# Gated channel tiles in pairs, five buffers for them, and a first block product fed in halves

## The chip, the cores and the metric

The kernel runs on one core of a Trainium2 chip. The metric is the device time of one execution in microseconds (us). The engines are TensorE (PE, matrix multiply), VectorE (DVE), ScalarE (ACT), GpSimd (POOL) and SyncE (SP, which only issues transfers); ACT, POOL and SP each have a queue that issues DMA transfers in program order, and each engine runs its instructions in order.

## What is computed

One layer of a hybrid token mixer over 2048 tokens of 1024 channels. Cut to what matters here:

```python
h = rms_norm(x, norm_g) * (1 + scale) + shift
va, za, bb, bc, bv, zb, ca, cg, zc, dv, zd = split(h @ w_in, 11)      # 512 channels each
ya = rglru(va)                                  # A: two scans with gates
yb = bb * conv3(bc * bv)                        # B
u  = layer_norm(conv31(ca * sigmoid(cg)))       # C
yc = silu(u) @ c_pw + c_pw_b
yd = (pool_grid(dv) @ d_w + d_b) * d_scale      # D
cat = concat([ya * silu(za), yb * silu(zb), yc * silu(zc), yd * silu(zd)])
x = x + gate * (cat @ w_out)
return rms_norm(x, final_g)
```

## The kernel before

Tokens are cut into four blocks of 512 (block b), channels into tiles of 128. Every fp32 matmul operand is split into a high and a low part (`split`, L105 to L108: the high part on ACT, the low part on DVE), and three matmuls of 128x128 by 128x512 make one product of parts. An input projection of one channel tile over one block is thus 24 matmuls into one of four PSUM accumulators (pool `pm`). `load_w` brings a tile's weights through the pool `wst` (two slots) and splits them into `wh` and `wl` (pool `wp`, three slots each).

The order of groups is written out in `JOBS`: A to D are the mixers' branches, a lower-case letter is a gated ("z") tile of that branch, F is `finish_c(b)` for one block, G and X, Y are other parts. Behind the list the last two z tiles run together with `project_two`. A scheduler with a simulated clock and priorities (`tc.high_priority(offset=URGENT)`) sets from it the order on each engine and the slot of each tile.

A z tile (`gated`, L461) takes silu of the accumulator on ACT into `sz` (L467), loads the branch's output `yt` on SP's queue (L472), multiplies on DVE (L473) and stores the product to DRAM on POOL's queue (`to_cat`, L455), even tiles into `first`, odd ones into `second`. The output projection is done as seven block products (a Strassen form), which need sums of even and odd tiles' halves. So an odd tile loads its even partner back (`yp`, L477), makes four sums (L479 to L482) in place, and stores them with two transfers (`to_sums`, L459). `sz`, `yt` and `yp` come from the pool `z2` with three slots, 512 floats wide.

`finish_c` (L765) does the layer norm of branch C for one block: it loads `uc`, gets the column mean by a matmul with a constant (`column_mean`: mups L790, and varps for the variance), takes the square root on ACT and the reciprocal on DVE, silu for four pieces, and then 48 matmuls with c_pw (pwps, L814). The first call loads c_pw (`pws`) on ACT's queue through `wst` into four `l4` tiles. The split mean operand `hl` stands in the pool `acc`.

Each of the seven products (L964 on: order 1, 2, 6, 7, 4, 5, 3) runs eight tiles of 24 matmuls (`q`, L995). The right operand `wo` is made of eight pieces (`wos`, `right`), each loaded through `wst`; those of product 1 are requested on ACT's queue (L909), the others on SP's. The left operand of a tile is one load of 512 KB into an `l4` tile (`load_left`, L930), three tiles ahead, and a split into `ahl`. `TILES` orders the eight tiles; tile p belongs to block p // 2. The last steps of the kernel add the residual and normalise.

Of the kernel before, what the change touches and what calls it, by code (L numbers as in the profile page):

```python
# [8 lines left out]
F32 = mybir.dt.float32  # L9
F32R = mybir.dt.float32r  # L10
# [34 lines left out]
def flow_backbone_kernel(  # L45
# [265 lines left out]
    def load_w(slot, q, spare=False, sub=None):  # L311

        col = slot * W + q * P
        res = []
        with tc.high_priority(offset=URGENT):
            for hf in range(2):
                ws = wst_p.tile([P, 4, P], F32, tag="wst", name="ws")
                r = hf * 512
                nc.sync.dma_start(ws, w_in[0, r : r + 512, col : col + P].rearrange("(k p) e -> p k e", p=P))
                if spare and hf == 1:  # L320
                    both = acc_p.tile([P, 2, 4, P], F32R, tag="acc", name="whl")
                    wh, wl = both[:, 0], both[:, 1]
                else:
                    wh = wp.tile([P, 4, P], F32R, tag="wh", name="wh")
                    wl = wp.tile([P, 4, P], F32R, tag="wl", name="wl")
# [24 lines left out]
    def project_two(jobs, before=lambda b: None):  # L350

        ws = [load_w(slot, q, j == 1, nc.gpsimd if len(hb) == 1 else None) for j, (slot, q, _) in enumerate(jobs)]
        for b in range(NB):
# [107 lines left out]
    def gated(g, q):  # L461

        ch = 4 * "abcd".index(g) + q

        def one(b, ps):
            sz = z2("sz")
            nc.scalar.activation(sz, ps, AF.Silu)  # L467
            if g == "c":
                nc.gpsimd.dma_start(y_d[g, q][b // 2][:, 512 * (b % 2) : 512 * (b % 2 + 1)], sz)
                return  # L470
            yt = z2("yt")
            nc.sync.dma_start(yt, y_d[g, q][b // 2][:, 512 * (b % 2) : 512 * (b % 2 + 1)])  # L472
            nc.vector.tensor_tensor(sz, sz, yt, op=MUL)  # L473
            to_cat(b, ch, sz)
            if ch % 2:
                yp = z2("yp")
                nc.sync.dma_start(tokens(yp), first_d[b][:, :, ch // 2, :])  # L477
                x1, y1, x2, y2 = yp[:, :256], yp[:, 256:], sz[:, :256], sz[:, 256:]
                nc.vector.tensor_tensor(yt[:, :256], x1, y1, op=ADD)  # L479
                nc.vector.tensor_tensor(y1, y1, y2, op=ADD)  # L480
                nc.vector.tensor_tensor(x1, x1, y1, op=ADD)
                nc.vector.tensor_tensor(yt[:, 256:], x1, x2, op=ADD)  # L482
                to_sums(b, ch // 2, yp, yt)

        return one

# [278 lines left out]
    def finish_c(b):  # L765
        if not pw:
            for i in range(NQ):
                ws = wst_p.tile([P, W], F32, tag="wst", name="pws")
                load = nc.scalar.dma_start(ws, c_pw[0, i * P : (i + 1) * P, :])
                follow(load, last_act[0], "the tiles of the recurrence are free after its last block")  # L770
                t = l4("pw", F32R, (P, 2, W))
                nc.scalar.activation(t[:, 0, :], ws, AF.Copy)
                nc.vector.tensor_tensor(t[:, 1, :], ws, t[:, 0, :].bitcast(F32), op=SUB)
                pw.append(t)
        if True:
# [6 lines left out]
            def column_mean(name, src, t):  # L782
# [47 lines left out]
            for dst, p0, p1 in ((s3, x1, y1), (s1, y1, y2), (s2, s1, x1), (s4, s2, x2)):  # L830
                nc.vector.tensor_tensor(dst, p0, p1, op=ADD)
# [11 lines left out]
    def z(g, q):  # L843
        project(Z[g], q, gated(g, q))
# [25 lines left out]
    project_two([(ZD, 3, gated("d", 3)), (ZA, 3, gated("a", 3))])  # L870
# [31 lines left out]
    def right(i):  # L902
# [4 lines left out]
        def one(k):  # L907
            ws = wst_p.tile([P, 512], F32, tag="wst", name="wos")
# [58 lines left out]
    TILES = (4, 5, 0, 1, 6, 7, 2, 3)  # L967
    todo = [(i, p) for i in ORDER for p in TILES]
    ats = [load_left(LEFT[i], p) for i, p in todo[:AHEAD]]
    for n, i in enumerate(ORDER):  # L970
# [4 lines left out]
        for m, p in enumerate(TILES):  # L975
            at = ats.pop(0)
            if 8 * n + m + AHEAD < len(todo):
# [75 lines left out]
```

## Time and profile before

| what | us |
|---|---|
| median of three runs | 1530.59 |
| lowest and highest run | 1526.68, 1532.86 |
| the profiled execution | 1526.85 |
| its span in the trace | 1524.9 |
| PE busy, DVE busy, ACT busy, POOL busy | 1453.0, 1116.2, 662.1, 166.7 |
| stretch of z tiles and finish_c, from the first pwps to the first product | 960.0 to 1201.3 |
| the seven products | 1201.3 to 1516.0 |

A time in the trace counts from the start of the span; the profiled execution's own time is 1.95 us longer than its span. "Busy" is the share in which an engine has an instruction under way; a pipelined matmul that follows another adds less than its own duration. A wait is put down to the instruction or transfer that ended it. The stretch of the table was found by the lines: L814 is pwps and L995 the products.

### The profile page before, as it was taken

How to read it: one execution, taken by the hardware profiler on the slowest of the kernel's cores; microseconds unless marked ns; L12 is line 12 of the kernel's file. 1: busy time of each engine (PE TensorE's matmuls, PEld its weight loads, DVE VectorE, ACT ScalarE, POOL GpSimd, SP SyncE). 2: the span in 40 equal slices, each digit the busy share in tenths (PEclk: the TensorE clock that was granted, in tenths of full speed). 3: DMA queues.
4: the chain of work that ended last, by engine and by line, in shares of the span. 5: the costliest groups of instructions: out<-in, count | busy, mean ns of one | idle time of the engine just before them, and what ended most of it. 6: DMA issues, size and time to landing. Idle time of an engine off the chain costs nothing.

```text
span 1524.9 us, 17881 instructions
## 1 busy us (share of the span) xinstructions
PE 1453.0 (95%) x6457; PEld 1184.8 (78%) x6457; DVE 1116.2 (73%) x1573; ACT 662.1 (43%) x949; POOL 166.7 (11%) x290
## 2 busy tenths in 40 slices
PE   5999999999999999999999999979999699999997
PEld 3778888888888888888878887857877587788886
DVE  6889984869966999988844976464547446766897
ACT  7773475543144541343635345332424233333432
POOL 0200000000100000111111001323222210000000
PEclk9999999999999999999999999989999899999999
DMA  9312121322311223223243126646566968775674
GB/s 370 122 52 81 49 87 58 104 89 71 112 38 48 84 69 111 96 102 124 90 159 111 62 97 207 205 147 234 172 215 225 331 200 272 255 233 175 212 251 152
DMA packets 157308, 223.88 MB, mean 147 GB/s; under 512 B 16283, under 2 KB 98211, under 8 KB 157220
## 3 DMA queue, kind: packets, MB, share of 16 engines
q1 hardware_dynamic: 135836, 154.29, 31.9%
q0 software_dynamic: 19648, 65.31, 11.1%
q10 hardware_dynamic: 1736, 3.15, 0.7%
q8 instruction: 50, 0.82, 0.2%
q14 instruction: 38, 0.31, 0.1%
HBM read 149.29 MB, written 73.40 MB: 146 GB/s over the span
## 4 chain that ended last, share of the span: by engine, by line
PE 63%; issue 17%; DMA 11%; POOL 3%; DVE 3%; SPq 1%; ACT 1%; POOLq 0%; DVEq 0%; ACTq 0%
PE ps L342 44%; PE q L995 12%; PE gps L411 3%; PE ps L359 2%; DMA yp<-first 2%; DMA sums<-yp 2%; DMA yt<-yb 2%; SPq L132 1%; POOL sums L459 1%; DMA wos<-in_w_out_dram 1%; DMA sums<-yt 1%; DMA ws<-in_w_in_dram 1%; PE dps L758 1%; PE psc L636 1%; DMA yt<-ya 1%
## 5 line engine op out<-in xcount | busy, mean ns | idle before, releaser
L342 PE MATMUL ps<-hb,wh 128*128 128x512 f32 x2560 | 717.7, 395 | 11.5 <-ACT sz L467 10.8
L342 PEld LDWEIGHTS ps<-hb,wh 128*128 128x128 f32 x2560 | 483.2, 189 | 119.5 <-ACT sz L467 13.0
L342 PE MATMUL ps<-hb,wl 128*128 128x512 f32 x1280 | 411.7, 393 | 0.0
L995 PE MATMUL q<-wo,ahl 128*128 128x512 f32 x1344 | 308.8, 391 | 15.8 <-ACT sz L467 10.0
L995 PEld LDWEIGHTS q<-wo,ahl 128*128 128x128 f32 x1344 | 252.6, 189 | 72.0 <-ACT sz L467 10.4
L342 PEld LDWEIGHTS ps<-hb,wl 128*128 128x128 f32 x1280 | 242.0, 189 | 52.2 <-issue 1.7
L107 ACT ACTIVATE wh<-ws 128x512 fp32r<-128x512 f32 x94 | 58.6, 626 | 159.7 <-PE ps L342 141.6
L473 DVE TENSOR_TENSOR sz<-sz,yt 128x512 f32<-128x512 f32 x48 | 33.0, 687 | 92.3 <-DMA yt<-yd 30.7
L108 DVE TENSOR_TENSOR wl<-ws,wh 128x512 fp32r<-128x512 f32 x91 | 62.1, 684 | 30.2 <-ACT wh L107 30.0
L467 ACT ACTIVATE sz<-ps 128x512 f32<-128x512 f32 x64 | 36.9, 595 | 106.2 <-DVE yt L482 35.2
L539 DVE SCALAR_TENSOR_TENSOR cacc<-vc,csum,cacc 128x1024 f32<-128x1024 f32 x60 | 76.6, 1276 | 0.3
L525 DVE SCALAR_TENSOR_TENSOR cacc<-vc,pt,cacc 128x1024 f32<-128x1024 f32 x60 | 76.7, 1278 | 0.0
L417 ACT ACTIVATE gate<-gps,pt 128x512 f32<-128x512 f32 x64 | 40.9, 687 | 78.2 <-PE gps L411 78.1
L519 DVE SCALAR_TENSOR_TENSOR cb<-vc,pt,cb 128x1024 f32<-128x1024 f32 x56 | 71.8, 1282 | 0.0
L359 PE MATMUL ps<-hb,wh 128*128 128x512 f32 x192 | 64.0, 405 | 4.9 <-ACT sz L467 4.0
L107 ACT ACTIVATE wo<-wos 128x512 fp32r<-128x512 f32 x56 | 34.5, 628 | 69.5 <-DVE wos L913 40.6
L397 DVE SCALAR_TENSOR_TENSOR xc<-va,pt,xc 128x1024 f32<-128x1024 f32 x48 | 61.3, 1277 | 0.2
L913 DVE TENSOR_TENSOR wos<-wos,wot 128x512 f32<-128x512 f32 x40 | 26.8, 690 | 33.2 <-DMA wos<-in_w_out_dram 19.2
L108 DVE TENSOR_TENSOR wo<-wos,wo 128x512 fp32r<-128x512 f32 x56 | 37.3, 687 | 16.5 <-ACT wo L107 15.8
L107 ACT ACTIVATE ahl<-s 128x1024 fp32r<-128x1024 f32 x32 | 33.5, 1054 | 36.3 <-PE q L995 31.3
L426 DVE SCALAR_TENSOR_TENSOR xc<-xc,gate 128x1024 f32<-128x1024 f32 x16 | 19.6, 1224 | 40.6 <-ACT xc L425 40.5
L359 PEld LDWEIGHTS ps<-hb,wh 128*128 128x128 f32 x192 | 36.4, 193 | 13.6 <-ACT sz L467 4.8
(255 smaller groups left out, 1874.1 us busy)
## 6 DMA issues: line engine op xcount, KB each, us to landing
ws<-in_w_in_dram SPq DMA_DIRECT2D x96, 256.0 KB
s<-sums SPq DMA_DIRECT2D x32, 512.0 KB
wos<-in_w_out_dram SPq DMA_DIRECT2D x40, 256.0 KB
wot<-in_w_out_dram SPq DMA_DIRECT2D x40, 256.0 KB
modw<-in_mod_w_dram SPq DMA_DIRECT2D x8, 1024.0 KB
a<-second SPq DMA_DIRECT2D x16, 512.0 KB
xo<-in_x_dram SPq DMA_DIRECT2D x32, 256.0 KB
out_dram<-ys SPq DMA_DIRECT2D x32, 256.0 KB
```

The lines of the kernel that those rows point to most:

```text
L107: nc.scalar.activation(hi, src, AF.Copy)
L108: (sub or nc.vector).tensor_tensor(lo, src, hi.bitcast(F32), op=SUB)
L342: nc.tensor.matmul(ps[u], lhsT=wk, rhs=hb[2 * pr + u][:, k, part, :], start=(k == 0 and n == 0), stop=(k == NK - 1 and n == 2),)
L359: nc.tensor.matmul(ps, lhsT=wk, rhs=hb[b][:, k, part, :], start=(k == 0 and n == 0), stop=(k == NK - 1 and n == 2),)
L397: nc.vector.scalar_tensor_tensor(xc, v[:, o + k : o + k + n], par(w0 + k, q), xc, op0=MUL, op1=ADD)
L411: nc.tensor.matmul(ps, lhsT=w[:, 2 * d + g, :], rhs=xx[:, u : u + m], start=(i == 0), stop=(i == len(terms) - 1))
L417: nc.scalar.activation(dst[:, u : u + m], ps, AF.Sigmoid, bias=par(bias, q))
L467: nc.scalar.activation(sz, ps, AF.Silu)
L519: nc.vector.scalar_tensor_tensor(bb, x1[:, 1 + j : 1 + j + n], odd(j), bb, op0=MUL, op1=ADD)
L525: nc.vector.scalar_tensor_tensor(acc, x0[:, j : j + n], even(j), acc, op0=MUL, op1=ADD)
L539: nc.vector.scalar_tensor_tensor(acc, x1[:, 1 + j : 1 + j + n], csum[:, q, j : j + 1], acc, op0=MUL, op1=ADD)
L995: nc.tensor.matmul(ps, lhsT=hl[:, a, k, :], rhs=wo[:, k, w, :], start=(k == 0 and e == 0), stop=(k == NK - 1 and e == 2))
```

## The change

A z tile of the branches A, B and D no longer stands alone: `z` projects two channel tiles (even and odd) with `project_two`, block after block. The even tile's `sz` and `yt` stay in SBUF until the odd tile of the same block has its product; `pair_sums` then writes the four sums into the two `yt` tiles and reads the two `sz`. No `yp` is loaded. `z2` has five slots. The `wh` and `wl` tiles have four slots, and the spare weight tile in `acc` is gone. `JOBS` is reordered: the pair b0 stands where a single tile of it stood later, the tiles of C move, finish_c runs in the block order F0, a0, F1, F2, F3, and the last pair is a2 with a3. The column mean's two split halves and the four `pws` loads share tiles `gwh` and `gwl` of the pool `gp`, and `pws` is requested on SP's queue. The pieces of product 1's right operand go through `z2` instead of `wst`. Product 1's left operands are loaded as two halves of 256 KB through `wst` and split into `wh` and `wl`; the other products load as before. `TILES` is 0 to 7.

```diff
 JOBS = (
-    "X0 Y0 c0 G6 B0 G1 G5 A0 D1 b0 G3 G0 C1 B1 A1 G7 G2 C2 c1 c2 G4 A2 C3 b1 B2 D0 D2 c3 A3 d0 D3 B3 a0 "
-    "F2 d1 F0 a1 b2 F3 F1 a2 b3 d2"
+    "X0 Y0 c0 G6 B0 G1 G5 A0 D1 c1 G3 G0 C1 B1 A1 G7 G2 C2 b0 G4 A2 C3 c2 B2 D0 D2 c3 A3 d0 D3 "
+    "B3 F0 a0 F1 F2 F3 b2 d2"
 )
+LAST = ("a", 2)
+BLOCKS = (0, 1, 2, 3)
...
-    wp = ctx.enter_context(tc.tile_pool(name="wp", bufs=3))
+    wp = ctx.enter_context(tc.tile_pool(name="wp", bufs=4))
...
-    zp = ctx.enter_context(tc.tile_pool(name="zp", bufs=3))
+    zp = ctx.enter_context(tc.tile_pool(name="zp", bufs=5))
...
+        def chunk(b, ps, e):
+            yt, sz = z2("yt"), z2("sz")
+            nc.sync.dma_start(yt, y_d[g, q + e][b // 2][:, 512 * (b % 2) : 512 * (b % 2 + 1)])
+            nc.scalar.activation(sz, ps, AF.Silu)
             nc.vector.tensor_tensor(sz, sz, yt, op=MUL)
-            to_cat(b, ch, sz)
-            if ch % 2:
-                yp = z2("yp")
-                nc.sync.dma_start(tokens(yp), first_d[b][:, :, ch // 2, :])
...
-                to_sums(b, ch // 2, yp, yt)
+            to_cat(b, ch + e, sz)
+            return yt, sz
+        def first(b, ps):
+            even[b] = chunk(b, ps, 0)
+        def second(b, ps):
+            (s21, s0), (s34, s1) = even.pop(b), chunk(b, ps, 1)
+            pair_sums(s21[:, 256:], s21[:, :256], s34[:, :256], s34[:, 256:], s0[:, :256], s0[:, 256:], s1[:, :256], s1[:, 256:])
+            to_sums(b, ch // 2, s21, s34)
...
+    def pair_sums(s1, s2, s3, s4, x1, y1, x2, y2):
+        for dst, p0, p1 in ((s1, y1, y2), (s2, s1, x1), (s3, x1, y1), (s4, s2, x2)):
+            nc.vector.tensor_tensor(dst, p0, p1, op=ADD)
...
-                ws = wst_p.tile([P, W], F32, tag="wst", name="pws")
-                load = nc.scalar.dma_start(ws, c_pw[0, i * P : (i + 1) * P, :])
+                ws = gp.tile([P, W], F32, tag=f"gw{'hl'[i % 2]}", name="pws")
+                nc.sync.dma_start(ws, c_pw[0, i * P : (i + 1) * P, :])
...
-                hl = acc_p.tile([P, 2, 512], F32R, tag="acc", name="hl")
+                hl = [gp.tile([P, 512], F32R, tag=f"gw{h}", name=f"h{h}") for h in "hl"]
...
-        project(Z[g], q, gated(g, q))
+            first, second = gated(g, q)
+            project_two([(Z[g], q, first), (Z[g], q + 1, second)], blocks=BLOCKS)
...
-    project_two([(ZD, 3, gated("d", 3)), (ZA, 3, gated("a", 3))])
+    z(*LAST)
...
-            ws = wst_p.tile([P, 512], F32, tag="wst", name="wos")
+            ws = z2("wos") if i == 1 else wst_p.tile([P, 512], F32, tag="wst", name="wos")
...
-    TILES = (4, 5, 0, 1, 6, 7, 2, 3)
+    TILES = [2 * b + t for b in BLOCKS for t in range(2)]
...
+    def left_parts(name, p):
+        res = []
+        for hf in range(2):
+            at = wst_p.tile([P, 4, P], F32, tag="wst", name="ah")
+            nc.sync.dma_start(at, left(name, p)[:, 4 * hf : 4 * hf + 4, :])
+            ah = wp.tile([P, 4, P], F32R, tag="wh", name="ahh")
+            al = wp.tile([P, 4, P], F32R, tag="wl", name="ahl")
+            split(ah, al, at)
+            res.append((ah, al))
+        return res
...
-    nc = _bacc.Bacc("TRN2", target_bir_lowering=False, num_devices=1)
+    nc = _bacc.Bacc("TRN2", target_bir_lowering=False, num_devices=1, dynamic_dma_scratch_size=8192)
```

What this does to the order on three engines at the end of the z tiles is shown in pieces of the instruction order. On PE, before, the last z tile (ps1_3_3: branch A's gate, tile 3, block 3) stands directly ahead of product 1, whose tiles q1_4, q1_5 and so on each run as 24 matmuls in one piece:

```order
L359 MATMUL ps1_3_3_8805<-hb3_917,wh_8523 128x512 x2
L359 MATMUL ps1_3_3_8805<-hb3_917,wl_8524 128x512
L359 MATMUL ps1_3_3_8805<-hb3_917,wh_8523 128x512 x2
L359 MATMUL ps1_3_3_8805<-hb3_917,wl_8524 128x512
L359 MATMUL ps1_3_3_8805<-hb3_917,whl_8529 128x512 x12
L995 MATMUL q1_4_8900<-wo1_8847,ahl_8897 128x512 x24
L995 MATMUL q1_5_8935<-wo1_8847,ahl_8932 128x512 x24
L995 MATMUL q1_0_8970<-wo1_8847,ahl_8967 128x512 x24
```

After, the variance matmuls of the last finish_c stand between, and q1_0 and q1_1 alternate by pieces of wo1:

```order
L358 MATMUL ps1_3_3_8769<-hb3_918,wh_8530 128x512 x2
L358 MATMUL ps1_3_3_8769<-hb3_918,wl_8531 128x512
L801 MATMUL varps_7806<-hh_7802,onesm_101 128x512
L801 MATMUL varps_7806<-hl_7803,onesm_101 128x512
L1031 MATMUL q1_0_8875<-wo1_8809,ahh_8846 128x512
L1031 MATMUL q1_1_8917<-wo1_8809,ahh_8865 128x512
L1031 MATMUL q1_0_8875<-wo1_8809,ahh_8846 128x512
L1031 MATMUL q1_0_8875<-wo1_8809,ahl_8847 128x512
L1031 MATMUL q1_1_8917<-wo1_8809,ahh_8865 128x512
L1031 MATMUL q1_1_8917<-wo1_8809,ahl_8866 128x512
L1031 MATMUL q1_0_8875<-wo1_8809,ahh_8846 128x512
```

So product 1 begins with two tiles side by side, and the 48 pwps matmuls of the last finish_c stand further down, between the tiles of product 1.

On ACT, before, wo1's pieces are requested (L909) and split (L107) four z tiles ahead of the last one, sz_8596 being an earlier tile's silu:

```order
L467 ACTIVATE sz_8596<-ps1_3_0_8571 128x512
L909 DMA wos_8856<-in_w_out_dram 128x512
L909 DMA wos_8860<-in_w_out_dram 128x512
L107 ACTIVATE wo1_8847<-wos_8856 128x512
L909 DMA wos_8864<-in_w_out_dram 128x512
L107 ACTIVATE wo1_8847<-wos_8860 128x512
L909 DMA wos_8868<-in_w_out_dram 128x512
L107 ACTIVATE wo1_8847<-wos_8864 128x512
L820 ACTIVATE uc_7933<-pwps_7980,pt_149 128x2x256
```

After, the first piece is requested behind the last z tile's silu (sz_8795), and the next ones behind a table load and the square root of finish_c (us_7785 from varps):

```order
L478 ACTIVATE sz_8795<-ps1_3_3_8769 128x512
L923 DMA wos_8810<-in_w_out_dram 128x512
L110 ACTIVATE hh_7802<-us_7785 128x512
L110 ACTIVATE ahh_8871<-ah_8869 128x512
L110 ACTIVATE wo1_8809<-wos_8810 128x512
L110 ACTIVATE wo2_8856<-wos_8859 128x512
L811 ACT_TABLE_LOAD
L811 ACTIVATE us_7785<-varps_7806,fixed_130 128x512
L923 DMA wos_8814<-in_w_out_dram 128x512
L923 DMA wos_8818<-in_w_out_dram 128x512
L110 ACTIVATE wo2_8856<-wos_8901 128x512
L923 DMA wos_8822<-in_w_out_dram 128x512
```

The requests of product 1's right operand have moved from ahead of the last z tiles to behind them, in between steps of finish_c.

On SP's queue, before, each odd z tile's yt is followed by a load of its even partner from first (yp), between loads for finish_c (zt) and for product 2 (wos):

```order
L472 DMA yt_8559<-yd3_0_203 128x512
L477 DMA yp_8563<-first0_217 128x4x128
L472 DMA yt_8598<-ya3_0_179 128x512
L477 DMA yp_8602<-first0_217 128x4x128
L818 DMA zt_8029<-yc2_0_193 128x512
L472 DMA yt_8637<-yd3_0_203 128x512
L818 DMA zt_8047<-yc3_0_195 128x512
L909 DMA wos_8893<-in_w_out_dram 128x512
L477 DMA yp_8641<-first1_218 128x4x128
```

After, only yt loads are left of the z tiles, and product 1's halves (ah) and product 2's pieces (wos_8859) stand among them:

```order
L790 DMA uc_7780<-u2_215 128x2x256
L790 DMA uc_7780<-u3_216 128x2x256
L477 DMA yt_8726<-ya3_1_180 128x512
L477 DMA yt_8763<-ya2_1_178 128x512
L923 DMA wos_8859<-in_w_out_dram 128x512
L477 DMA yt_8794<-ya3_1_180 128x512
L990 DMA ah_8863<-first0_217 128x512
L990 DMA ah_8869<-first0_217 128x512
```

The yp loads are gone from the queue, and the left operands come in halves of 128x512.

## Rows read from the trace of the kernel before

**Rows 1.** Page: span, busy time of PE, and the group of wo's low-half splits.
```profile
span 1524.9 us, 17881 instructions
...
PE 1453.0 (95%) x6457; PEld 1184.8 (78%) x6457; DVE 1116.2 (73%) x1573; ACT 662.1 (43%) x949; POOL 166.7 (11%) x290
...
L108 DVE TENSOR_TENSOR wo<-wos,wo 128x512 fp32r<-128x512 f32 x56 | 37.3, 687 | 16.5 <-ACT wo L107 15.8
```

**Rows 2.** Windows of PE: us, busy (matmuls), granted clock, DMA share, GB/s.
```profile
40.00:960.00 920.00, 910.73 (x4088) 1.00 0.28 93
960.00:1201.30 241.30, 210.71 (x871) 0.94 0.64 218
1201.30:1516.00 314.70, 308.76 (x1344) 1.00 0.69 225
```

**Rows 3.** Timeline of PE: start, us, matmuls, [idle before <- what ended it].
```profile
1018.00 1.22 PE L342 MATMUL ps<-hb,wh 128*128 128x512 f32 x2 [3.54 <-ACT sz L467]
...
1184.20 1.22 PE L359 MATMUL ps<-hb,wh 128*128 128x512 f32 x2 [3.74 <-ACT sz L467]
...
1201.33 7.15 PE L995 MATMUL q<-wo,ahl 128*128 128x512 f32 x24 [9.96 <-ACT sz L467]
...
1331.13 149.21 PE L995 MATMUL q<-wo,ahl 128*128 128x512 f32 x657 [0.44 <-DVE ahl L108]
```

**Rows 4.** Waits of PE, 900 to 1350 us: us in total, times, longest.
```profile
PE ps L342 <- ACT sz L467: 10.8, 5, 3.5
PE q L995 <- ACT sz L467: 10.0, 1, 10.0
...
PE ps L359 <- ACT sz L467: 4.0, 2, 3.7
PE mups L790 <- DVE hl L108: 3.0, 2, 2.6
PE mups L790 <- ACT hl L107: 2.0, 2, 1.4
```

**Rows 5.** Waits of SyncE's DMA queue, 900 to 1330 us.
```profile
SPq L472 <- DMA sums<-yp: 74.6, 18, 7.5
```

**Rows 6.** Windows of PE, 10 us each, columns as in rows 2.
```profile
1010.00:1020.00 10.00, 6.46 (x25) 0.83 0.39 133
1190.00:1200.00 10.00, 1.37 (x7) 0.71 1.05 405
```

**Rows 7.** Chain that ended last, 1180 to 1210 us: start, us, what.
```profile
1184.20 7.18 PE ps L359 x24
```

**Rows 8.** Timeline of ACT, columns as in rows 3.
```profile
1131.59 0.33 ACTq L909 DMA_DIRECT2D wos<-in_w_out_dram  x1
...
1142.30 1.28 ACT L800 ACT_TABLE_LOAD   x1
1143.59 0.69 ACT L800 ACTIVATE us<-varps,fixed 128x512 f32<-128x512 f32 x1
...
1151.66 0.80 ACT L804 ACTIVATE uc<-uc,pt 128x512 f32<-128x512 f32 x1
...
1155.76 0.60 ACT L467 ACTIVATE sz<-ps 128x512 f32<-128x512 f32 x1
...
1165.40 0.34 ACTq L909 DMA_DIRECT2D wos<-in_w_out_dram  x1
...
1167.26 0.33 ACTq L909 DMA_DIRECT2D wos<-in_w_out_dram  x1
1168.43 0.63 ACT L107 ACTIVATE wo<-wos 128x512 fp32r<-128x512 f32 x1 [0.84 <-DMA wos<-in_w_out_dram]
1171.84 0.63 ACT L107 ACTIVATE wo<-wos 128x512 fp32r<-128x512 f32 x1 [2.77 <-DMA wos<-in_w_out_dram]
...
1192.49 1.25 ACT L107 ACTIVATE wo<-wos 128x512 fp32r<-128x512 f32 x2 [5.59 <-DMA wos<-in_w_out_dram]
```

**Rows 9.** Timeline of SyncE's queue, around the same transfer.
```profile
1183.25 1.00 SPq L909 DMA_DIRECT2D wos<-in_w_out_dram  x2
```

More of the change, by code (lines that the diff above doesn't have):

```diff
@@ L308, in prepare_block, with load_w @@
         hb.append(t)
-    def load_w(slot, q, spare=False, sub=None):
+    def load_w(slot, q, sub=None):
         col = slot * W + q * P
@@ L319, in load_w @@
                 nc.sync.dma_start(ws, w_in[0, r : r + 512, col : col + P].rearrange("(k p) e -> p k e", p=P))
[L320 to L325, printed above, removed]
+                wh = wp.tile([P, 4, P], F32R, tag="wh", name="wh")
+                wl = wp.tile([P, 4, P], F32R, tag="wl", name="wl")
                 split(wh, wl, ws, sub)
@@ L348, in project, with project_two @@
                     evac(2 * pr + u, ps[u])
-    def project_two(jobs, before=lambda b: None):
-        ws = [load_w(slot, q, j == 1, nc.gpsimd if len(hb) == 1 else None) for j, (slot, q, _) in enumerate(jobs)]
-        for b in range(NB):
+    def project_two(jobs, before=lambda b: None, blocks=range(NB)):
+        ws = [load_w(slot, q, nc.gpsimd if len(hb) == 1 else None) for slot, q, _ in jobs]
+        for b in blocks:
             before(b)
@@ L785, in column_mean @@
                 nc.vector.tensor_tensor(t[:, :512], t[:, :512], t[:, 512:1024], op=ADD)
-                hl = acc_p.tile([P, 2, 512], F32R, tag="acc", name="hl")
-                split(hl[:, 0, :], hl[:, 1, :], t[:, :512])
+                hl = [gp.tile([P, 512], F32R, tag=f"gw{h}", name=f"h{h}") for h in "hl"]
+                split(hl[0], hl[1], t[:, :512])
                 ps = aux_ps(name)
                 for i in range(2):
-                    nc.tensor.matmul(ps, lhsT=onesm, rhs=hl[:, i, :], start=(i == 0), stop=(i == 1))
+                    nc.tensor.matmul(ps, lhsT=onesm, rhs=hl[i], start=(i == 0), stop=(i == 1))
                 return ps
@@ L843, in z @@
     def z(g, q):
-        project(Z[g], q, gated(g, q))
+        if g == "c":
+            project(ZC, q, silu_c(q))
+        else:
+            first, second = gated(g, q)
+            project_two([(Z[g], q, first), (Z[g], q + 1, second)], blocks=BLOCKS)
     run = {
@@ L988, in flow_backbone_kernel @@
                 one(m)
-            hl = mid_t("ahl", (P, 2, 8, P), F32R)
-            with tc.high_priority(offset=URGENT):
-                split(hl[:, 0], hl[:, 1], at)
+            if at is None:
+                if 8 * n + m + 1 < FIRST:
+                    parts.append(left_parts(LEFT[i], TILES[m + 1]))
+                part = parts.pop(0)
+                lefts = [[part[k // 4][a][:, k % 4, :] for k in range(NK)] for a in range(2)]
+            else:
+                hl = mid_t("ahl", (P, 2, 8, P), F32R)
+                with tc.high_priority(offset=URGENT):
+                    split(hl[:, 0], hl[:, 1], at)
+                lefts = [[hl[:, a, k, :] for k in range(NK)] for a in range(2)]
             ps = main_ps(f"q{i}_{p}")
@@ L995, in flow_backbone_kernel @@
                     nc.tensor.matmul(
-                        ps, lhsT=hl[:, a, k, :], rhs=wo[:, k, w, :], start=(k == 0 and e == 0), stop=(k == NK - 1 and e == 2)
+                        ps, lhsT=lefts[a][k], rhs=wo[:, k, w, :], start=(k == 0 and e == 0), stop=(k == NK - 1 and e == 2)
                     )
```

32 lines of the change are left out of this document (13 added, 19 removed).

## The prediction, before the changed kernel ran

> **What bounds the kernel now.** I read the page first: TensorE (PE) is busy 1453.0 of 1524.9 us [rows 1], so only time that PE loses can be won. Next came the windows of PE over three stretches [rows 2]. From 40 to 960 us PE is busy 910.73 of 920.00 us at a granted clock of 1.00, and nothing is left there. From 960.0 to 1201.3 us (the z tiles and the four blocks of finish_c) it is busy 210.71 of 241.30 us, and the clock is 0.94 of full speed. From 1201.3 to 1516.0 us (the seven block products) it is busy 308.76 of 314.70. What a full-speed matmul of 512 columns costs is read from a long run without gaps: 657 in 149.21 us [rows 3], 0.227 us each. So the 871 matmuls of the middle stretch are 197.5 us of work in 241.3 us: 43.8 us lost, 30.6 of them idle (241.3 - 210.7) and 13.2 slow (210.7 - 197.5). The 1344 matmuls of the products are 304.7 us of work, and 10.0 us are lost in 314.7.
>
> The waits of PE say on what [rows 4]. **z evacuation**: an accumulator is not free because silu (ACT, L467) has not read it: 10.8 us in L342 and 4.0 in L359, of which one wait of 3.74 stands directly before the products [rows 3], and 10.0 at the first product. ACT itself waits there for a z2 slot: each odd z tile holds three of the three slots (sz, yt, yp) until two stores of sums have landed, and SyncE's queue (SPq) loses 74.6 us to exactly that, 18 waits of up to 7.5 us [rows 5]. **finish_c**: 3.0 + 2.0 us for the column mean's split.
>
> The slow part has its own look. Behind a wait the matmuls come two in 1.22 us, at 1018.00 and at 1184.20 [rows 3], where two at full speed are 0.62 us; the granted clock is 0.83 of full speed in the 10 us around the first [rows 6]. Idle PE is followed by PE at the lower of its two levels (1.2 instead of 2.4 GHz).
>
> **Part 1, z tiles in pairs, five slots, sums from SBUF.** Removed: 24 loads of yp (256 KB each, 6.3 of 223.9 MB), and with them the round trip store-load-add that held three slots. Multiplies, adds and stores stay as many. A pair holds sz and yt of both tiles: four slots out of five. In the slot order that the program is built with, the even sz of the next pair finds the fifth slot free, and only the odd tile waits for a store of sums of the pair before. PE needs 2 x 24 x 0.227 = 10.9 us for a pair; the waits for that store were 7.5 us at the longest [rows 5], and four PSUM accumulators stand between. So I take all of 10.8 + 0.26 (4.0 less 3.74) = **11.1 us** as gained. Bounds: 0, if stores are as late as now and the odd tile only takes the even one's place; and 11.1. The nearest row, the wait of 7.5 against 10.9, is well on the good side.
>
> **Part 2, the clock.** Of 13.2 us slow, 1.6 belong to the 24 matmuls at 1184.20 (7.18 us [rows 7] against 5.6 at full speed) and are counted in part 3. Of the other 11.7 I take half, **6 us**, since the finish_c waits lie in the same 40 us and stay. Bounds 0 and 11.7.
>
> **Part 3, start of the first product.** Before, it loses 3.74 + 1.6 (above) + 9.96 + 1.55 (7.15 us for 24 [rows 3]) + 0.7 = 17.5 us. All of wo1 was ready 30 us ahead (first request 1131.59, last split 1171.84 [rows 8]) and the cause was z slots. After, wo1's eight pieces go through z2 on ACT's queue, and the order puts the first request behind the last silu, and the next seven behind the table load and square root of the last finish_c, which now falls into the first product. I chain that by rows, T being the end of the last z matmul: silu 0.60, load 3.0 (1165.40 to 1168.43), split 0.63 on ACT and 0.69 on VectorE [rows 8, 1]: first product matmul at about T+5. ACT then splits a piece of wo2, loads its table 1.28, takes the square root 0.69, and requests the others from T+7.8 to T+16.0, each with its load and a split in between; the last is in use at T+16 + 3.0 + 1.3 = T+20. In this time PE has two matmuls of varps and 48 of q1_0 and q1_1, 11.3 us: some 9 us lost. Behind the last request stand a table load and silu (0.80) and split (0.63) for each of four pieces of finish_c, 1.4 apart, so its pwps matmuls run from T+20.4 to about T+30 with nothing else ahead in PE's order, against 16.8 us of matmuls up to there: 13.2 us lost, and 1 to 3 for the lower clock. I take **15**, a gain of 2.5. Who waits for the first wo1 piece: PE, all of product 1; behind the waiting splits on ACT: the square root and so finish_c. Bounds: 5 (only the first piece shows) and 30 (all loads as the slow one: requested 1183.25, used 1192.49, 9.2 us [rows 8, 9]). Most loads of this size took 3.0 to 4.6 (1167.26 to 1171.84), hence the value near the low rows.
>
> The loads of before were done 30 us ahead of use [rows 8], and without its z waits product 1 would have lost 2.2 us (17.5 - 3.74 - 9.96 - 1.6). A rule of the Trainium skill speaks against the move: "DMA: Bandwidth & Descriptors", section "Rules for kernel authors", wants a transfer issued early and waited for late. By the rows of before alone the start would gain 15.3, and by this rule the late requests give back all but the 2.5 of the chain above; no row of before shows a late one.
>
> **Part 4, left operands in halves.** Sixteen halves of 256 KB instead of eight tiles of 512 KB, through two wst slots that also carry wo2. From T on about 18 loads are left for two slots. A turn is load 3.0 + split 1.3 + request 0.5 = 4.8 us, so 9 turns are 43 us; PE needs 192 + 48 matmuls, 54 us, plus its 15 of waiting. Cost 0 beside that cover. For a 256 KB load the rows show 3.0 to 4.6 us. The Trainium skill's page "DMA: Bandwidth & Descriptors", section "Anatomy of one DMA — SWDGE (gpsimd) path", gives 2.0 us fixed plus the bytes at 436 GB/s, an estimate of 2.6 us for a half and 3.2 for a whole; by it the halves would cost 2.0 us more a tile, 8 us over two slots and eight tiles, still inside the cover, and the measured 3.0 is what the sum uses.
>
> **Part 5, finish_c waits.** Splits go to two tiles, the c_pw loads to SP, and the last block into product 1: 5.0 us become 4, **1** gained. Bounds -11 (third rival) and 5.
>
> **Part 6, the rest.** The products lose 7.7 us beyond their start; block order 0 to 3 and SPq's order (requests for zt, wos and xo behind one another) change which wait shows. I take **1 us worse**; bounds -4 and +5. Before 960 us jobs move, a fourth weight slot replaces the spare one, PE is full [rows 2]: 0, bound 4 worse.
>
> Sum on the profiled execution: 11.1 + 6 + 2.5 + 1 - 1 = 19.6 us. It took 1526.85 us, so 1507.3. The median of the three runs is 1530.59, 3.74 above that execution: **1511.0 us**.
>
> **Rivals.** *Better: the start hides itself.* Requests are accepted while ACT waits elsewhere, varps is early, and only the first piece shows: 5 instead of 15 lost, 1501. For it: wo1 needs only 2 MB and the last pair no yp. Against: ACT's queue is strictly in order. If the clock is gained whole too, 1495.
>
> *Slower: two wst slots set the pace of product 1.* If each load takes the 9.2 us of [rows 8, 9], nine turns of 9.2 + 1.3 + 0.3 are 97 us from T, against 54 of matmuls: 43 lost where 17.5 were lost before, 25.5 worse. With 18.1 gained elsewhere less the 1 of part 6: 8.4 worse, **about 1539**. It decides from about 8.3 us a load, where nine turns eat the gain. For it: the window 1190 to 1200 us has DMA at 1.05 busy and 405 GB/s [rows 6]. Against: that burst carried the prefetched left tiles and yp, which are gone; part 4's 6 MB in 60 us are 100 GB/s.
>
> *No change: finish_c takes the place of the z tiles.* The chain sum, mean, square, mean, root must now fit between fewer z matmuls; if each of four blocks waits as the longest of before (2.6 + 1.4 [rows 4]), that is 16 us instead of 5, and the clock stays low: 19.6 - 12 - 6 = 1.6 gained, **1529**. For it: PE passes only 33 matmuls, 7.5 us, between the last mean and its variance. Against: the three earlier blocks have 51 to 64, 12 to 14 us.
>
> **How the numbers follow.** Forecast 0.52 (1511, own range 1504 to 1519), better 0.22, no change 0.16, slower 0.10. The range runs from 1495 (better, with the clock) to 1530 (no change); beyond it lie the slower rival and a little on the low side. A measurement of this kernel tells about 0.5% (7.7 us) from no change, so faster means under 1522.9: 0.50 of the forecast, 0.22, and 0.02 of the third rival, 0.74; slower means over 1538.2: 0.09; the rest is 0.17.
>
> **What would show it.** Part 1: waits of L359 on the silu line near 0 between 960 and 1190 us; no row sums<-yp; if they stay, the slots still bind. Part 2: granted clock above 0.97 in the z stretch. Part 3: PE idle at the first product under wo<-wos (ACT or VectorE split), 5 us and then several of 1 to 4 us, first product matmul 5 us behind the last z matmul; pwps waiting for uh. Part 4: waits on ahl of under 2 us in product 1; many of them mean the slower rival. Part 5: mups and varps waits of 4 us in all; over 12 mean the third. The prediction is wrong if the stretch to the first product keeps 30 us idle, or if product 1 takes over 85 us instead of about 70.

## The result, and the profile after

The changed kernel takes 1511.93 us (median of four runs, 1510.03 to 1517.37) against 1530.91 of the kernel before in the same comparison; the ratio is 0.9887 with a 95% interval of 0.9865 to 0.9908. A second comparison of the same pair (r1 below) gave 1512.27 against 1528.47, ratio 0.9900 (0.9879 to 0.9920). The forecast was 1511.0. The number was met. One step of the sum behind it failed, and part of what covered for it is luck: two other steps gave more than forecast, and the profiled executions stand differently to their medians.

The profiled execution of the changed kernel took 1517.37 us. Its page:

```profile
span 1515.6 us, 17854 instructions
...
PE 1453.5 (96%) x6457; PEld 1185.0 (78%) x6457; DVE 1117.1 (74%) x1581; ACT 664.4 (44%) x959; POOL 164.9 (11%) x290
```

PE is busy as long as before [rows 1], so in this execution the gain is all idle time. Where it went is read from the same three windows of both kernels (columns as in [rows 2]); the kernel before first, the changed one second:

```profile
500.00:930.00 430.00, 429.31 (x1882) 1.00 0.30 101
930.00:1150.00 220.00, 202.41 (x836) 0.95 0.59 198
1150.00:1300.00 150.00, 130.72 (x557) 0.95 0.77 261
```

```profile
500.00:930.00 430.00, 417.48 (x1805) 0.99 0.30 100
930.00:1150.00 220.00, 217.93 (x951) 1.00 0.61 204
1150.00:1300.00 150.00, 133.68 (x547) 0.94 0.72 241
```

In the z stretch PE's idle time fell from 17.6 us to 2.1 and the granted clock rose from 0.95 to 1.00. Ahead of it, where the kernel before loses 0.7 us, the changed one loses 12.5. Around the start of the products the idle time fell by 3 us (19.3 to 16.3), and the clock is 0.94 instead of 0.95. The waits of PE from 500 to 1350 us say on what (columns as in [rows 4]):

```profile
PE gps L410 <- ACT xh L110: 6.0, 1, 6.0
PE q L1031 <- ACT ahh L110: 5.1, 3, 1.8
PE varps L801 <- ACT hh L110: 4.1, 1, 4.1
PE q L1031 <- ACT wo L110: 3.7, 2, 2.2
PE ps L341 <- ACT sz L478: 2.6, 2, 1.7
PE mups L801 <- ACT hh L110: 2.3, 2, 1.5
PE ps L358 <- ACT sz L478: 1.9, 1, 1.9
```

None of the two sz lines lies behind 930 us: the waits of [rows 4] on the silu, 24.8 us in all, are gone from the z stretch and from the first product, and 4.5 us of such waits are new ahead of it, where z tiles now stand among the recurrences. The first line is new. It is the gate matmul (gps) of branch A's recurrence, which stands at the head of PE's order until its input xh is split, so PE has nothing else to run. PE's row (timeline, columns as in [rows 3]) shows the lower clock behind it, two matmuls in 1.22 us:

```profile
867.96 1.22 PE L410 MATMUL gps<-xh,gwh 128*128 128x512 f32 x2 [6.00 <-ACT xh L110]
```

The start of product 1, from the same timeline:

```profile
1169.52 0.49 PE L801 MATMUL varps<-hh,onesm 128*128 128x512 f32 x1 [4.09 <-ACT hh L110]
...
1172.26 1.94 PE L1031 MATMUL q<-wo,ahh 128*128 128x512 f32 x3 [1.51 <-ACT wo L110]
...
1187.32 0.73 PE L825 MATMUL pwps<-uh,pw 128*128 128x512 f32 x2 [1.26 <-ACT uh L110]
...
1224.72 0.73 PE L1031 MATMUL q<-wo,ahh 128*128 128x512 f32 x2 [1.71 <-ACT ahh L110]
...
1234.70 0.73 PE L1031 MATMUL q<-wo,ahh 128*128 128x512 f32 x2 [1.53 <-ACT ahh L110]
```

The last z matmul ends at 1165.4 us. Product 1 starts 6.8 us later, the last finish_c's pwps 21.9 us later. The requests for wo1 on ACT's queue come as late as the instruction order has them, the first beside the last silu and the others beside and behind the table load:

```profile
1167.04 0.37 ACTq L923 DMA_DIRECT2D wos<-in_w_out_dram  x1
...
1172.74 1.28 ACT L811 ACT_TABLE_LOAD   x1
1172.78 0.94 ACTq L923 DMA_DIRECT2D wos<-in_w_out_dram  x2
...
1182.77 0.33 ACTq L923 DMA_DIRECT2D wos<-in_w_out_dram  x1
```

### The profile page after: what moved, and what is told of

The parts are those of the page before. It is cut to its first block, busy times and chain, and to the rows that moved or that the text cites. A ratio compares the mean times of both kernels' runs of the same rounds, so it can differ in the third digit from the quotient of the medians.

```text
span 1515.6 us, 17854 instructions
## 1 busy us (share of the span) xinstructions
PE 1453.5 (96%) x6457; PEld 1185.0 (78%) x6457; DVE 1117.1 (74%) x1581; ACT 664.4 (44%) x959; POOL 164.9 (11%) x290
## 3 DMA queue, kind: packets, MB, share of 16 engines
q0 software_dynamic: 19648, 65.31, 11.1%
## 4 chain that ended last, share of the span: by engine, by line
PE 60%; issue 17%; DMA 7%; DVE 6%; ACT 3%; POOL 2%; SPq 0%; DVEq 0%; POOLq 0%; ACTq 0%
PE ps L341 32%; PE q L1031 12%; PE ps L358 10%; PE gps L410 2%; PE pwps L825 2%; DMA dvr<-dv 1%; DMA wos<-in_w_out_dram 1%; PE psc L646 1%; DVE cacc L535 1%; DMA ws<-in_w_in_dram 1%; DVE cb L529 1%; DMA uc<-u 1%; DMA sums<-us 1%; POOL sums L458 1%; DMA sums<-yt 1%
## 5 line engine op out<-in xcount | busy, mean ns | idle before, releaser
L341 PE MATMUL ps<-hb,wh 128*128 128x512 f32 x1920 | 525.3, 392 | 2.6 <-ACT sz L478 2.6
L341 PEld LDWEIGHTS ps<-hb,wh 128*128 128x128 f32 x1920 | 360.8, 188 | 79.8 <-ACT sz L478 3.4
L341 PE MATMUL ps<-hb,wl 128*128 128x512 f32 x960 | 301.0, 390 | 0.0
L1031 PE MATMUL q<-wo,ahl 128*128 128x512 f32 x1216 | 289.1, 391 | 0.1
L358 PE MATMUL ps<-hb,wh 128*128 128x512 f32 x896 | 285.2, 396 | 2.8 <-ACT sz L478 1.9
L1031 PEld LDWEIGHTS q<-wo,ahl 128*128 128x128 f32 x1216 | 229.3, 189 | 50.1 <-DVE ahl L111 2.4
L341 PEld LDWEIGHTS ps<-hb,wl 128*128 128x128 f32 x960 | 180.5, 188 | 37.9 <-issue 0.2
L358 PEld LDWEIGHTS ps<-hb,wh 128*128 128x128 f32 x896 | 168.5, 189 | 41.7 <-ACT sz L478 2.7
L358 PE MATMUL ps<-hb,wl 128*128 128x512 f32 x448 | 175.9, 393 | 0.0
L358 PEld LDWEIGHTS ps<-hb,wl 128*128 128x128 f32 x448 | 84.5, 189 | 19.0 <-issue 1.7
L425 DVE SCALAR_TENSOR_TENSOR xc<-xc,gate 128x1024 f32<-128x1024 f32 x16 | 19.6, 1225 | 52.2 <-ACT xc L424 52.0
L1031 PE MATMUL q<-wo,ahh 128*128 128x512 f32 x128 | 45.4, 433 | 9.2 <-ACT ahh L110 5.1
```

What stands on the lines that cost most here:

```text
L341: nc.tensor.matmul(ps[u], lhsT=wk, rhs=hb[2 * pr + u][:, k, part, :], start=(k == 0 and n == 0), stop=(k == NK - 1 and n == 2),)
L358: nc.tensor.matmul(ps, lhsT=wk, rhs=hb[b][:, k, part, :], start=(k == 0 and n == 0), stop=(k == NK - 1 and n == 2),)
L1031: nc.tensor.matmul(ps, lhsT=lefts[a][k], rhs=wo[:, k, w, :], start=(k == 0 and e == 0), stop=(k == NK - 1 and e == 2))
```

## The experiments

All medians are of runs beside the kernel before, whose medians in these comparisons were 1526.9 to 1528.5 us. Every edit of the source lets the scheduler place the instructions around it anew, so each run was also read by its own waits. Idle and slow time of a stretch are read as in the prediction: idle is the stretch less PE's busy time, slow is the busy time less 0.2267 us for each matmul (the value behind the prediction's 197.5 us for 871).

**r1, the changed kernel again.** No edit.

> The changed kernel as it is, beside the others of this call. Theory (the profiled run's gaps are in the order of the instructions, not chance): 1509 to 1514 us, and again some 9 us of idle PE between 800 and 900 us (one gap of 6 before gps, waiting for xh), some 10 us idle between the last z tile and 1215 us and some 5 us under the halves' high parts (ahh) in product 1. Rival (the profiled run, 1517.4, was an odd one): the gap before gps is under 1 us in this profile.

Measured 1512.27 us. The profile of another execution (1512.20 us) has the same gaps: 5.5 us before gps, 4.8 at varps, 5.7 under ahh. They belong to the order, not to chance.

**r2, only the slots.**

```diff
-    zp = ctx.enter_context(tc.tile_pool(name="zp", bufs=3))
+    zp = ctx.enter_context(tc.tile_pool(name="zp", bufs=5))
...
-    nc = _bacc.Bacc("TRN2", target_bir_lowering=False, num_devices=1)
+    nc = _bacc.Bacc("TRN2", target_bir_lowering=False, num_devices=1, dynamic_dma_scratch_size=8192)
```

> The kernel before with five z2 slots instead of three and nothing else (single z tiles, yp loads, old order of jobs, old feed of product 1); the smaller ring for DMA descriptors makes the room. Theory A (slots alone do it; the pairs only save traffic): the waits of PE on the z silu fall from 25 us to under 5, the first product starts without its wait of 10, and the time is 1500 to 1512, as good as the changed kernel. Theory B (the round trip store, load, add is what takes the time, and slots only shift it): 10 us or more of silu waits stay, 1518 to 1528.

Measured 1498.60 us, ratio 0.9813 (0.9793 to 0.9832): 14 us faster than the changed kernel. PE's waits from 500 to 1350 us:

```profile
PE q L995 <- ACT ahl L107: 7.5, 3, 5.3
PE mups L790 <- ACT hl L107: 6.0, 1, 6.0
PE ps L342 <- ACT wh L107: 3.1, 1, 3.1
```

No line on the silu is left, with single tiles and with every yp load still there. The two more slots alone remove the silu waits of [rows 4] (not those of finish_c, which are 7.7 us here instead of 5.0). Beside five slots the rest of the change, taken together, costs 14 us. The smaller ring for DMA descriptors (the second line of the edit) makes the room and was not run alone; r11 has it too.

**r11, one slot more.** The same edit with bufs=4.

> The kernel before with four z2 slots instead of three, nothing else. Theory A (one odd single tile holds three slots, so one more slot lets the next silu go ahead and is most of what r2 won): 1498 to 1506. Theory B (both more slots are needed): 1510 to 1520 with 8 us or more of silu waits.

Measured 1516.62 us, ratio 0.9914. Theory B holds: silu waits of 9.4 us stay, and one weight wait of 4.4 us joins them. With the smaller ring in both runs, the step from four to five slots is 18 us by the medians (some 15 by the ratios); the first slot and the ring together are 11 (13).

```profile
PE q L995 <- ACT ahl L107: 9.5, 2, 7.0
PE ps L342 <- ACT sz L467: 9.4, 3, 5.2
PE ps L359 <- DVE wl L108: 5.3, 2, 4.4
```

**r3, pairs with four slots.**

```diff
-    zp = ctx.enter_context(tc.tile_pool(name="zp", bufs=5))
+    zp = ctx.enter_context(tc.tile_pool(name="zp", bufs=4))
```

> The changed kernel with four z2 slots instead of five, everything else as in its source. Theory A (the fifth slot lets the even silu of the next pair go ahead of the stores of sums): silu waits of PE of 5 to 15 us come back between 960 us and the last z tile, 1517 to 1530. Theory B (four PSUM accumulators cover the stores anyway): within 3 us of the changed kernel.

Measured 1510.88 us, as the changed kernel. No silu wait stands behind 930 us; one of 7.6 us stands at 534 us. It is made up elsewhere (no gap before gps, a shorter start of product 1). From 500 to 930 us PE still idles 12.4 us, as in the changed kernel, but for other things: this silu wait and one of 4.5 us for a weight of branch D. For the z stretch the pairs do not need the fifth slot.

**r7, the pairs undone.** The changed kernel with its list of jobs, slots and feed:

```diff
-            first, second = gated(g, q)
-            project_two([(Z[g], q, first), (Z[g], q + 1, second)], blocks=BLOCKS)
+            project(Z[g], q, gated1(g, q))
+            project(Z[g], q + 1, gated1(g, q + 1))
```

where gated1 is the function of before, with its yp load.

> The changed kernel with its list of jobs, five slots and its feed of product 1, but each pair done as two single z tiles, the second loading its partner back (yp, 24 loads of 256 KB) as in the kernel before. It undoes the pairing alone. Theory A (pairing itself is worth little once there are five slots): 1507 to 1517, within 5 us of the changed kernel. Theory B (sums from SBUF are what frees the z stage): silu waits of 10 us or more come back, 1520 to 1530.

Measured 1524.82 us, 12.6 slower than r1: theory B's time without its mechanism. The waits on the silu are 0.6 us; most of what came is finish_c:

```profile
PE pwps L851 <- ACT uh L110: 10.1, 1, 10.1
PE mups L827 <- ACT hh L110: 9.6, 3, 4.7
```

VectorE and ACT run finish_c's steps in one queue with the z tiles' multiplies and sums. VectorE's timeline shows the sum of a block (us from uc) held until 1021.09 us, which the profile puts down to a store of a z tile's product; the second half of that sum and the split for mups stand behind it, and a mups wait of 3.8 us:

```profile
1021.09 1.22 DVE L820 TENSOR_TENSOR us<-uc 128x1024 f32<-128x1024 f32 x1 [4.91 <-DMA first<-sz]
```

So the pairs are worth about 12 us in this list of jobs, and by these waits they earn it mostly in finish_c's chain. Ahead of 930 us r7 idles less than r1 (6.5 us against 12.0), but more than the kernel before (0.7): single tiles do not close the hole that the new list has there. That the yp transfers are the reason is the nearest reading of these rows (an odd tile's adds wait for a load of what was just stored); the runs do not separate it from the other changes of order.

**r4, the old feed of product 1.**

```diff
-            ws = z2("wos") if i == 1 else wst_p.tile([P, 512], F32, tag="wst", name="wos")
+            ws = wst_p.tile([P, 512], F32, tag="wst", name="wos")
...
-    FIRST = 8
-    parts = [left_parts(LEFT[1], p) for _, p in todo[:1]]
+    FIRST = 0
+    parts = []
+    ats = [load_left(LEFT[i], p) for i, p in todo[:AHEAD]]
```

> The changed kernel with product 1 fed as before: left operands in whole 512 KB tiles through l4, wo1's pieces through wst; requests still on ACT's queue; the order of the z tiles and finish_c stays. Theory A (the halves pay: l4 is held by c_pw until the last finish_c is done, so product 1 would start late): product 1's first matmul stands 20 us or more behind the last z tile, PE idle there 15 to 30 us instead of 10, time 1515 to 1530. Theory B (late requests of wo1 through z2 are what costs at the start): the start loses less than in the changed kernel, 1503 to 1510.

Measured 1523.79 us, 11.5 slower than r1. The idle time that theory A wanted is there, 25.0 us behind the last z tile (7.7 of the mups line, the other two, and a wait of 4.5 on ahl beside them):

```profile
PE pwps L825 <- ACT uh L110: 8.7, 1, 8.7
PE mups L801 <- ACT hh L110: 8.3, 2, 7.7
PE varps L801 <- ACT hh L110: 4.1, 1, 4.1
```

With the old feed product 1 starts behind the last finish_c, whose c_pw tiles hold l4 (its first matmul stands at 1206.04 us, the last of pwps at 1201.07), and so every step of that finish_c shows.

**r5, the halves alone on top of r2.** left_parts and its use as in the change, FIRST = 8, with five slots in the kernel before.

> The kernel before with five z2 slots (as r2) and, on top, only product 1's left operands in halves through wst, wh and wl (three slots each); jobs, single tiles, yp loads, wo1 through wst and tile order as before. Theory A (halves pay only where l4 is still held by c_pw, that is, where the last finish_c ends inside product 1; here it ends ahead of it): within 3 us of r2 (1498.6), at most the 5.3 us wait on the first left operand goes. Theory B (halves are better wherever product 1 starts): 1485 to 1493, as 11.5 us were won between r4 and r1.

Measured 1521.94 us, 23.3 slower than r2. Neither theory had this sign. The waits on the left operand are now 18.4 us in four pieces:

```profile
PE q L1017 <- ACT ahh L107: 18.4, 4, 6.5
```

Sixteen halves and eight pieces of wo2 share two wst slots and three wh slots. Three of the halves that ACT waits for take 8.2 to 8.8 us from request to split, the first of them here:

```profile
1183.71 0.32 SPq L976 DMA_DIRECT2D ah<-first  x1
1191.95 0.63 ACT L107 ACTIVATE ahh<-ah 128x512 fp32r<-128x512 f32 x1 [5.16 <-DMA ah<-first]
```

The slower rival of the prediction needed about 8.3 us a load. So this is its mechanism, in another kernel; whether one wh slot more (the changed kernel has four) would ease it was not run.

**r6, an earlier finish_c.**

```diff
-    "X0 Y0 c0 G6 B0 G1 G5 A0 D1 c1 G3 G0 C1 B1 A1 G7 G2 C2 b0 G4 A2 C3 c2 B2 D0 D2 c3 A3 d0 D3 "
-    "B3 F0 a0 F1 F2 F3 b2 d2"
+    "X0 Y0 c0 G6 B0 G1 G5 A0 D1 c1 G3 G0 C1 B1 A1 G7 G2 C2 G4 A2 C3 c2 B2 D0 D2 c3 A3 b0 D3 B3 F0 d0 F1 F2 F3 a0 b2 d2"
```

> The changed kernel with another list of jobs: the pairs b0 and d0 go behind the last recurrence (A3), where b0 is the fill and d0, a0, b2, d2 follow; nothing else changed. The last gate matmul of the recurrence then stands about 120 matmuls (27 us) earlier in PE's order and the last finish_c ends ahead of product 1 instead of inside it. Theory A (the late finish_c is what the pairs' job list costs): the wait of varps (4.8) and of pwps (2.3) goes, 1498 to 1506. Theory B (the pieces of wo1, still requested behind the last z tile, cost the same alone): 1508 to 1514 with 8 us or more of PE waiting on wo at the first product.

Measured 1523.37 us, outside both ranges. My list took away b0 where PE needed it as fill:

```profile
PE ps L340 <- ACT vc L513: 20.2, 1, 20.2
PE q L1030 <- ACT wo L109: 11.4, 3, 8.1
```

The first line (at 546 us, about where b0 stood) is an accident of the list and hides the question by time. The waits answer it in part: varps and pwps are gone, as theory A had it, but the late pieces of wo1 now show alone, with 11.4 us (theory B), and the start of product 1 is no better. The Trainium skill's page "DMA: Bandwidth & Descriptors", section "Rules for kernel authors", asks to issue early and wait late; the trace agrees, since with the early requests of the old feed (r8) no wait on wo is left. There the first piece is requested at 1129.81 us, in r6 at 1184.41, and the first matmul of product 1 stands at 1192 us in both. What r8 waits for instead is the left operand, 9.2 us.

**r8, r6 with the old feed.** The edit of r4 on r6.

> r6 with product 1 fed as before (whole left operands through l4, wo1 through wst). With r1, r4 and r6 it closes a square: late or early finish_c, old or new feed. Theory A (the old feed is bad only because l4 is held): within 4 us of r6 or better than it, 1496 to 1506, since wo1 is requested early again. Theory B (the old feed costs 11 us wherever finish_c ends): 11 us slower than r6.

Measured 1516.84 us, 6.5 faster than r6, with the same gap of 20.2 us, which keeps it above theory A's range; the sign is theory A's. So the feed of product 1 has no price of its own:

| last finish_c | new feed | old feed |
|---|---|---|
| ends inside product 1 (r1, r4) | 1512.3 | 1523.8 |
| ends ahead of it (r6, r8; each with the gap of 20.2) | 1523.4 | 1516.8 |

r3 is a second case of the lower left cell, without that gap: in its order the last pwps ends at 1174.4 us, product 1 stands behind it with the new feed, and it took 1510.9 (with four z2 slots). From 500 to 930 us r6 idles 24.6 us and r3 12.4; less this difference r6 would be at 1511.2 too. By these sums the place of the last finish_c is worth almost nothing with the new feed (1512.3 against about 1511), and it is the old feed that needs it early.

**r9 and r10, the two good parts together.** The changed kernel with the list of before up to B3 and pairs only behind it ("+" marks a pair; the other z tiles are single ones, by r7's gated1), and the old feed (edit of r4). r9:

```diff
-    "X0 Y0 c0 G6 B0 G1 G5 A0 D1 c1 G3 G0 C1 B1 A1 G7 G2 C2 b0 G4 A2 C3 c2 B2 D0 D2 c3 A3 d0 D3 "
-    "B3 F0 a0 F1 F2 F3 b2 d2"
+    "X0 Y0 c0 G6 B0 G1 G5 A0 D1 b0 G3 G0 C1 B1 A1 G7 G2 C2 c1 c2 G4 A2 C3 b1 B2 D0 D2 c3 A3 d0 D3 B3 F0 d1 F1 F2 F3 a0+ b2+ d2+"
```

> The changed kernel with the list of jobs of before up to B3 (b0, b1 and d0 as single z tiles with a load of the partner, so that the last recurrence ends as early as before), then F0, d1, F1, F2, F3 and the pairs a0, b2, d2 and last a2; product 1 fed as before (whole left operands, wo1 through wst). Theory A (pairs are good behind the recurrence and cost where they delay it; the old feed suits a finish_c that ends ahead of product 1): no gap over 2 us between 500 and 930 us, z stage under 5 us idle, start of product 1 7 to 12 us idle, 1486 to 1496, faster than r2 (1498.6). Theory B (pairs bring nothing over singles with five slots): 1497 to 1505.

Measured 1500.61 us (1498.57 to 1503.65). In r10 the list behind B3 reads "a0 F0 d1 F1 a1 F2 F3 b2+ d2+".

> As r9, but a0 and a1 stay single z tiles (F0, d1, F1, a1, F2, F3 behind a0): only b2, d2 and a2 are pairs. Theory A of r9: one pair fewer, 0 to 4 us slower than r9. Theory B: as r9 within 2 us.

Measured 1497.00 us (1490.90 to 1499.81), ratio 0.9780 (0.9743 to 0.9816). The idle time ahead of 930 us is 0.4 to 0.5 us in both, but the gain over r2 is small or none: r9 misses theory A and falls in theory B's range. r10 is 3.6 us faster than r9, which neither of its theories had, and the ranges of r9, r10 and r2 meet, so the runs do not tell the three apart with certainty. The largest wait left in r10 is the one at product 1:

```profile
PE q L1059 <- ACT ahl L109: 9.1, 2, 7.5
PE pwps L850 <- ACT uc L856: 4.0, 1, 4.0
PE mups L826 <- ACT hh L109: 4.0, 2, 2.4
```

SyncE's queue shows the reason: the first left operand is requested at 1166.60 us, as c_pw's tiles come free (the chain that ended last has the pwps matmuls up to 1166.60 us directly ahead of this load), and is split at 1173.55.

```profile
1166.60 0.39 SPq L971 DMA_DIRECT2D a<-first  x1
```

```profile
1173.55 1.06 ACT L109 ACTIVATE ahl<-a 128x1024 fp32r<-128x1024 f32 x1 [5.76 <-DMA a<-first]
```

**r12, halves where they are needed.** r10 with the first two tiles of product 1 in halves:

```diff
-    FIRST = 0
-    parts = []
-    ats = [load_left(LEFT[i], p) for i, p in todo[:AHEAD]]
+    FIRST = 2
+    parts = [left_parts(LEFT[1], p) for _, p in todo[:1]]
+    ats = [load_left(LEFT[i], p) for i, p in todo[FIRST:AHEAD]]
```

> r10 (late pairs, a0 and a1 single, old feed) with the first two tiles of product 1 alone in halves through wst, wh and wl; the other six tiles through l4, wo1 through wst. In r10 product 1 waits 7.5 us for its first left operand, whose load was requested at 1166.60 us, as the last pwps gave l4 free. Theory A (that is the whole of this wait): it falls to under 2 us and the clock behind it stays up, 1486 to 1493. Theory B (as in r5 the two wst slots are short: halves push wo1 and wo2 back): waits on ahh or on wo of 6 us or more in its place, 1495 to 1505.

Measured 1484.12 us (1480.42 to 1484.82), ratio 0.9717 (0.9693 to 0.9741): 12.9 us below r10 and 28 below the changed kernel, a little better than theory A's range. It is faster than the kernel before and than the changed one. The first half is now requested at 1132.18 us, and matmuls of product 1 run between the pwps from 1152.38 on. From 1150 to 1300 us PE idles 4.3 us instead of r10's 13.8, and slow time falls from 6.3 to 1.7. That is more than the operand's wait alone, since the waits of pwps shrank too. All of PE's waits of 1 us or more from 500 to 1350 us:

```profile
PE q L1059 <- ACT ahl L109: 1.8, 1, 1.8
PE q L1059 <- DVE ahl L110: 1.5, 2, 1.4
PE mups L826 <- ACT hh L109: 1.5, 1, 1.5
PE pwps L850 <- ACT uh L109: 1.5, 2, 1.0
PE gateT L906 <- ACT uc L856: 1.0, 1, 1.0
```

## Why the prediction was right, and where it was not

The direction and the time were right, the time in part by luck. The sum was made from profile to profile, 19.6 us, and there it is too high: the profiled execution of after is 9.5 us shorter than that of before (1526.85 to 1517.37), that of r1 14.7 (1512.20). By medians it is 19.0 (16.2 in the second comparison): the profiled execution of before stands 4.1 us below its median, that of after 5.4 above. Step by step, in us gained, in the profile of after:

| step | predicted | measured |
|---|---|---|
| 1, silu waits of the z stretch | 11.1 | 11.1 |
| 2, clock of the z stretch | 6 | 9.1 |
| 3, start of product 1 | 2.5 | 2.1 |
| 4 and 6, rest of the products | -1 | -0.7 |
| 5, mups in the z stretch | 1 | 2.7 |
| 6, before 960 us (measured 500 to 930) | 0 | -11.8 idle, -5.6 slow |

The last row is worked out from the first windows of the two kernels above: 429.31 us for 1882 matmuls are 2.7 us slow, 417.48 us for 1805 are 8.3. The measured column adds up to 6.9; the other 2.6 of the 9.5 lie outside these stretches or at their edges. What is measured behind 930 us rests on these windows:

```profile
930.00:1159.00 229.00, 225.41 (x983) 1.00 0.61 204
1159.00:1215.00 56.00, 46.30 (x179) 0.88 0.66 214
1215.00:1250.00 35.00, 29.91 (x117) 0.95 0.67 222
1250.00:1506.00 256.00, 255.93 (x1130) 1.00 0.69 227
```

- **Part 1 came as priced**, but its reason was half right. Slots are what bound (r2), yet the argument that pairs need the fifth slot fell: four do for the z stretch (r3). The prediction's own other reason, that four accumulators stand between, would explain it and is not shown. And a point was missing: nobody had to pair tiles to win this.
- **Part 2:** from 930 to 1159 us 983 matmuls take 225.41 us of busy time, 2.6 more than at full speed, instead of 11.7. I kept half back for finish_c's waits; of those only single ones of 0.75 and 1.53 us stay there, and the granted clock is 1.00. The 3.1 us here and the 1.7 of step 5 above their forecasts covered a part of what the last row lost.
- **Part 3, 15 us lost, measured 15.4:** 9.7 us idle from the last z matmul to the pwps, and 5.7 slow (46.30 us busy for 179 matmuls). The chain held in its times: requests at T+1.6 and T+7.3 to T+17.3 (predicted 7.8 to 16.0 for the later ones), first matmul T+6.8 (5), pwps T+21.9 (20.4). Two of its parts were wrong. Of the idle time 4.1 us are the wait of varps, which I had put at nothing, and the waits on wo are shorter for it. And the split was 13.2 idle with 1 to 3 slow: the idle time between pieces of pwps did not come, since pieces of q stand between them and PE loses nothing more from T+21.9 to 1215 us, while the lower clock cost 5.7 us instead of 1 to 3. That the two errors cancel is luck.
- **Part 4:** 0 was taken; 5.1 us idle under ahh and 3.4 slow (29.91 us for 117 matmuls) were measured. The cover was reckoned on nine even turns of 4.8 us in two slots. The rows below show one of 7.7, from a half's request over its split to the next request in the freed slot; the last six halves took 3.0 to 6.4 us from request to split, not 3.0 each. (The prediction's estimate of 2.6 us a half, from a fit for transfers on the GpSimd path, is further off; SyncE issues these.) Part 6's "1 us worse" met this only because nothing at all is lost behind 1250 us.

```profile
1217.68 0.32 SPq L990 DMA_DIRECT2D ah<-first  x1
...
1224.04 0.63 ACT L110 ACTIVATE ahh<-ah 128x512 fp32r<-128x512 f32 x1 [4.71 <-DMA ah<-first]
...
1225.42 0.32 SPq L990 DMA_DIRECT2D ah<-first  x1
```

- **Part 6, "before 960 us: 0, bound 4 worse", is the step that failed.** The stretch from 500 to 930 us is idle for 12.5 us (12.0 in r1) instead of 0.7, beyond the bound, and the clock between 800 and 900 us is 0.95. PE was full there [rows 2], and I took that as a reason that a new list of jobs would keep it so; it was full because the list fed it. r9, r10 and r12, with the list of before up to B3, have 0.4 to 0.5 us there; with the new list r3, r6 and r7 have 12.4, 24.6 and 6.5, each under other waits. The new list also ends the last recurrence later: its last gate matmul stands at 946.7 us (r1) instead of 910.3. In seven profiles (before, after, r1, r3, r6, r10, r12) the last variance matmul of finish_c follows that gate matmul by 216 to 227 us. So in the changed kernel it falls behind the last z tile and the rest of finish_c into product 1, while in r3 and r6, whose last gate matmul stands at 936.2 and 933.4, it stays ahead. I had seen the late finish_c in the instruction order and priced it, but had not asked for its cause.

Of the rivals, "finish_c takes the place" is the nearest to the truth in r7 and r4; "two wst slots set the pace" is real in r5 (23 us) and did not decide here: in the changed kernel the halves come sooner (3.0 to 6.4 us for the last six), and while the first ones come PE also has the matmuls of the last finish_c. Which of the two matters more was not tested.

What stays open: how the cost of the whole change beside the slots (1498.6 against 1512) divides between the list and the feed, since they act on one another; what the smaller descriptor ring does alone; and the moves of pws to SP and of hl to gp, which were not run alone.

## What to carry to other kernels

A pool that is short of buffers (here by two, for one more was not enough) looks like a problem of data flow: try the buffers alone before rebuilding the flow, and judge the rebuilt flow against that, not against the old kernel. A stretch in which the bounding engine is full is full for its present order; a change that moves jobs must be charged for the holes that it can open there, by asking what fills the engine at each long dependent chain. And a resource that is held by one stage until its end (here l4 by c_pw) sets what feed the next stage needs: bridge just the tiles that fall into that time.

## What was not expected of the hardware

Behind the gap of 6.00 us the first two matmuls take 1.22 us (at 867.96), the lower of the two levels, while behind the gap of 1.71 us at 1224.72 the first two take 0.73 us and those behind them run at full speed. The gap at 1234.70 is the third of its kind within 12 us; at 1229.84 too (1.83 us idle) full speed followed, but behind the third the matmuls run at the lower level from 1235.4 for some 4 us (granted clock 0.91 from 1230 to 1250 us). Which gaps cost the clock can't be read from their length alone in these rows.
